# The first mixer's 31-tap convolution as column-packed products on TensorE

## Chip, cores, metric

One core of one Trainium2 chip. The metric is the device time of one execution in microseconds (us), the median of several runs. The engines are TensorE (PE, its weight loads PEld), VectorE (DVE), ScalarE (ACT), GpSimd (POOL) and SyncE (SP, which issues nearly all DMA).

## What is computed

A decoder trunk of two layers on 512 tokens of 1024 features, float32. Layer 0 runs sliding-window attention and a Conformer convolution side by side, each on its part of one input projection; their outputs, 512 + 512 features, go through one output projection. A gated feed-forward with a short convolution follows; layer 1 is a state-space mixer with the same feed-forward. Every residual is modulated by vectors computed from a condition c. The part that the change concerns:

```python
def conformer_conv(u, conv_w, conv_b, ln_g, ln_b):
    a, g = jnp.split(u, 2, axis=-1)                        # 512 features each
    h = causal_dwconv(a * jax.nn.sigmoid(g), conv_w, conv_b)  # 31 taps per feature
    mu = jnp.mean(h, axis=-1, keepdims=True)
    var = jnp.mean(jnp.square(h - mu), axis=-1, keepdims=True)
    h = (h - mu) * lax.rsqrt(var + LN_EPS) * ln_g + ln_b
    return jax.nn.silu(h)

merged = jnp.concatenate([attn, conf], axis=-1)            # attn: 8 heads, window 128
x = x + g_m * (merged @ w_out)
```

## The kernel before

The residual `x` stays on chip, feature-major: 8 tiles of 128 features by 512 tokens. A dense product takes three passes in a rounded float32 form: weights and inputs are split into a head and a remainder, and head by head, head by remainder and remainder by head are summed in PSUM (`mm3`, `product`). Weight tiles of 128 x 1024 stream from DRAM in the order of use (`Stream`): SP loads (`raw`, three buffers), ACT makes the head (`head`), DVE or POOL the remainder (`rest`).

`even_layer` is the first mixer. First the norm and the modulation fill `hn`, and six PSUM banks `g0` take the input products for three of the four convolution tiles (values and gates). Then a planner takes over. `Plan` holds tasks, each with an engine, a cost in us, what it waits for and which buffers it takes and gives; whenever an engine of its model falls idle it emits the ready task with the highest rank, which is the longest chain of costs behind it plus a number from the table `MIXER0`. `plan.run(MIXER0)` so fixes the order of every engine's instructions and of the DMA issues. A task made by `either` may have several ways, on DVE or on POOL.

The plan covers: two products for the fourth convolution tile (a3, g3), the key, value and four query products; rotary steps on DVE; for each of four head pairs (`head_tasks`) two units of scores, maxima, exponents, transposes (`turn`), copies (`bring`) and values, then a merge; the convolution of four tiles; its layer norm (means, centring, squares, variances, `ln`, silu); the output projection, first its attention half for all eight feature tiles (`out_a`), then the convolution half for four of them (`out_c`); and beside it 24 modulation chunks (`plan_mods`), each a load of 128 x 1024 weights and a dot with the condition.

One convolution tile is 128 features x 512 tokens. `gated` makes its input `us`; the last tap starts `cv`; the other 30 taps are one task each: on DVE a multiply-add on `cv` with a shifted `us`, or on ACT a product and on POOL an add into `cv2`; `conv_sum` joins the two. The modulation dot is one DVE operation, or a POOL product and an ACT sum. The scores of a unit are built per kv group: a mask product, then two products on that group's 64 rows. After the plan `boundary` makes the last four feature tiles of the output projection, 256 tokens at a time, and the next phase's norm.

Of the kernel before, what the change touches and what calls it, by code (L numbers as in the profile page):

```python
# [16 lines left out]
F32 = mybir.dt.float32  # L17
# [50 lines left out]
SIDE_LAST = 20.0  # L68
# [7 lines left out]
MIXER0 = {'sigmoid': -25, 'square': 43, 'osq_add': 139, 'head': -111, 'tap0': -113, 'attn_h': -95, 'conv_h': 49, 'out_c': 138, 'gated': 6, 'rest': -110, 'values': 71, 'rope': 59, 'rstd': -51, 'mod_sum': 7, 'attn_l': 103, 'var': 150, 'turn': 139, 'mod_end': 90, 'exp': -81, 'bring': 30, 'conv_sum': 54, 'out_a': -98, 'osq': -83, 'mod_act': -104, 'mod_add': 39, 'mod_free': 120, 'normalize': 30, 'load': -25, 'product': -67, 'mean_row': -71, 'mod_dve': 105, 'tap': -30, 'recip': 12, 'ln': 23, 'centre': -33, 'residual': -119, 'maxima': 140, 'rstd_row': -150, 'conv_l': 97, 'mean': 47, 'rope_in': 80, 'v_bias': -29, 'mod_load': 105, 'mod_dot': -93, 'root': 30, 'rows': -61, 'rows_in': -80, 'v_turn': -20, 'v_in': 85, 'mod 2': 18, 'head 0': -16, 'mu': 62, 'keys': 64, 'conv 0': 4, 'head 1': 2, 'mod 1': -4, 'head 3': -14}  # L76
# [20 lines left out]
class Way:  # L97
    """One engine's way of doing a task; then is one more task that follows if this way is taken."""
# [109 lines left out]
def trunk(ctx: ExitStack, tc: tile.TileContext, xT_d, vecs_d, rows_d, dsk_d, pos_d, const_d, wss_d, wg0_d,  # L208
          w_d, wmod_d, wdt_d, out_d):
# [34 lines left out]
    # ------------------------------------------------------------------ constants and small inputs  # L244
# [28 lines left out]
    # ------------------------------------------------------------------ splitting and products  # L273
# [4 lines left out]
    class Stream:  # L278
        """The weight tiles in the order in which they are used: DMA runs furthest ahead, then the
        split into heads and remainders, then the products."""  # L280
# [45 lines left out]
        def plan(self, plan, count, bonus, more):  # L326
# [51 lines left out]
    def spread(col, n=NCH):  # L378
        """[128 tokens, n] -> [128 partitions, n * 128 tokens], the same on every partition."""
# [15 lines left out]
    def rstd_cols(ss, width, e=0, n=NCH):  # L395
        """(sum / width + eps) ** -0.5 per token: ACT's square root, reciprocal, one Newton step."""
# [17 lines left out]
    def modulator(G, sh):  # L414
        """The normed, modulated, split tiles of the next phase, and what fills one token half."""
# [118 lines left out]
    # ------------------------------------------------------------------ modulation  # L534
# [6 lines left out]
    def condition(cp):  # L541
        """silu(c) on every partition."""
# [79 lines left out]
    def even_layer(lp, cp):  # L622
# [1205 lines left out]
```

## Time and profile before

| | |
|---|---|
| median of 3 runs | 1429.57 us (1427.97 to 1430.26) |
| profiled execution: span | 1428.4 us |
| PE busy | 1333.0 us (93%) |
| DVE busy | 969.4 us (68%) |
| ACT busy | 612.8 us (43%) |
| POOL busy | 339.1 us (24%) |
| DMA, mean over the span | 125 GB/s |

The span runs from the first to the last instruction; the profile gives no other time of its own for this execution, and the median of the runs stands 1.2 us above it. The shares are averages over stages with different limits. The page's 40 slices of 35.7 us show two kinds: PE is at nine tenths or more from the eighth slice on, and lower, with DVE at nine tenths, in the third to sixth. Views of single stretches, of groups of instructions by line, of waits, and the timeline give what happens there.

### The profile page before, as it was taken

To read this page: it belongs to the slowest core of one execution; us is meant where nothing else is said; L and a number is where in the kernel's file an instruction comes from. 1 tells how busy PE (TensorE), PEld (TensorE's weight loads), DVE (VectorE), ACT (ScalarE), POOL (GpSimd) and SP (SyncE) were. 2 spreads that over 40 slices of the span, in tenths; PEclk is the share of its full clock that TensorE was granted. 3 is DMA by queue.
4 is the path that set the end of the run, shared out by engine and by line. 5 is a ranking of instruction groups with operands and counts; after the bars stand their busy time and mean duration, and the time that the engine had idled before them with its cause. 6 is when DMAs were issued, how large, how long until landed. Compare 5 with 4: busy or idle time off the path is not lost. (4 is left out here: it accounts for less than half of the span.)

```text
span 1428.4 us, 17187 instructions
## 1 busy us (share of the span) xinstructions
PE 1333.0 (93%) x6574; PEld 1096.4 (77%) x6575; DVE 969.4 (68%) x1406; ACT 612.8 (43%) x897; POOL 339.1 (24%) x230
## 2 busy tenths in 40 slices
PE   6958748999999999999997999989999999999997
PEld 5745436888888888888786777777898888888886
DVE  7899999777566566657697866876766434444543
ACT  4545755454223323336467263464544322322333
POOL 7875767100000000011344422433210000000002
PEclk8977869999999999999998999999999999999998
DMA  8632016337566465432342332333214223223221
GB/s 302 246 117 89 1 57 208 113 128 231 162 206 197 148 221 191 147 102 86 117 133 85 115 114 74 135 95 100 88 40 139 90 89 114 85 92 108 92 70 59
DMA packets 54305, 178.08 MB, mean 125 GB/s; under 512 B 6480, under 2 KB 11088, under 8 KB 54224
## 3 DMA queue, kind: packets, MB, share of 16 engines
q1 hardware_dynamic: 53504, 176.34, 38.2%
q8 instruction: 51, 0.84, 0.2%
q10 hardware_dynamic: 688, 0.66, 0.2%
q14 instruction: 30, 0.25, 0.0%
q0 software_dynamic: 32, 0.00, 0.0%
HBM read 174.81 MB, written 2.16 MB: 124 GB/s over the span
## 5 line engine op out<-in xcount | busy, mean ns | idle before, releaser
L350 PE MATMUL ps<-hn,wl 128*128 128x512 f32 (+1 forms) x1214 | 458.1, 377 | 9.4 <-DVE wl L302 9.2
L348 PE MATMUL ps<-hn,wh 128*128 128x512 f32 (+1 forms) x1214 | 464.1, 382 | 1.1 <-ACT hn L424 0.8
L349 PE MATMUL ps<-hn,wh 128*128 128x512 f32 (+1 forms) x1214 | 458.2, 377 | 0.4
L297 ACT CAST wh<-raw 128x1024 fp32r<-128x1024 f32 (+1 forms) x208 | 213.0, 1027 | 206.4 <-PE ps L349 178.4
L302 DVE TENSOR_TENSOR wl<-raw,wh 128x1024 fp32r<-128x1024 f32 (+1 forms) x170 | 216.2, 1275 | 93.4 <-ACT wh L297 92.5
L350 PEld LDWEIGHTS ps<-hn,wl 128*128 128x128 f32 x1214 | 231.0, 190 | 52.5 <-DVE wl L302 10.4
L348 PEld LDWEIGHTS ps<-hn,wh 128*128 128x128 f32 x1214 | 231.6, 191 | 44.9 <-issue 2.0
L349 PEld LDWEIGHTS ps<-hn,wh 128*128 128x128 f32 x1214 | 231.2, 190 | 43.0 <-issue 1.7
L412 POOL TENSOR_TENSOR ssq<-ssq,tmp 128x512 f32<-128x512 f32 x10 | 13.3, 1334 | 725.0 <-ACT tmp L411 725.0
L437 DVE SCALAR_TENSOR_TENSOR x<-ps,modv,x 128x512 f32<-128x512 f32 (+1 forms) x108 | 74.2, 689 | 125.5 <-PE ps L350 125.3
L348 PE MATMUL ps<-fh,wh 128*128 128x512 f32 (+1 forms) x380 | 142.2, 374 | 0.0
L349 PE MATMUL ps<-fl,wh 128*128 128x512 f32 (+1 forms) x380 | 141.9, 373 | 0.0
L350 PE MATMUL ps<-fh,wl 128*128 128x512 f32 (+1 forms) x380 | 141.9, 373 | 0.0
L302 POOL TENSOR_TENSOR wl<-raw,wh 128x1024 fp32r<-128x1024 f32 x38 | 94.5, 2488 | 167.5 <-ACT wh L297 156.6
L566 DVE SCALAR_TENSOR_TENSOR mr<-mr,cb 128x1024 f32<-128x1024 f32 x86 | 117.8, 1375 | 0.0
L811 POOL TENSOR_TENSOR mr<-mr,tmp 128x506 f32<-128x506 f32 (+26 forms) x55 | 79.3, 1453 | 37.3 <-ACT tmp L806 35.1
L1224 DVE SCALAR_TENSOR_TENSOR tmp<-ps,vecs,tmp 128x511 f32<-128x511 f32 x44 | 32.9, 749 | 79.9 <-ACT tmp L1223 79.9
L1223 ACT ACTIVATE tmp<-ps,vecs 128x512 f32<-128x512 f32 x44 | 34.3, 780 | 115.4 <-PE ps L350 115.4
L348 PEld LDWEIGHTS ps<-fh,wh 128*128 128x128 f32 x380 | 71.5, 188 | 12.8
L349 PEld LDWEIGHTS ps<-fl,wh 128*128 128x128 f32 x380 | 71.5, 188 | 12.6
L350 PEld LDWEIGHTS ps<-fh,wl 128*128 128x128 f32 x380 | 71.5, 188 | 12.6
L796 DVE SCALAR_TENSOR_TENSOR s<-s,vecs,s 128x503 f32<-128x503 f32 (+28 forms) x61 | 74.7, 1236 | 1.2
(283 smaller groups left out, 1732.3 us busy)
## 6 DMA issues: line engine op xcount, KB each, us to landing
raw<-in_w_dram SPq DMA_DIRECT2D x176, 512.0 KB, 3.6
mr<-in_wmod_dram SPq DMA_DIRECT2D x80, 512.0 KB, 3.6
raw<-in_w_dram SPq DMA_DIRECT2D x32, 448.0 KB, 3.4
mr<-in_wss_dram SPq DMA_DIRECT2D x16, 512.0 KB, 6.2
M<-scr SPq DMA_DIRECT2D x16, 512.0 KB, 4.4
raw<-in_wg_dram SPq DMA_DIRECT2D x8, 384.0 KB, 4.7
E<-scr SPq DMA_DIRECT2D x32, 96.0 KB, 3.6
x<-in_xT_dram SPq DMA_DIRECT2D x8, 256.0 KB, 4.7
```

The source lines that it names most:

```text
L297: nc.scalar.copy(h, self.raw[i].rearrange("p (k m) -> p k m", m=P))
L302: eng.tensor_tensor(l, self.raw[i].rearrange("p (k m) -> p k m", m=P), h.bitcast(F32), ALU.subtract)
L348: mm(ps, lhsT=w[0], rhs=ah, start=first, stop=False)
L349: mm(ps, lhsT=w[0], rhs=al, start=False, stop=False)
L350: mm(ps, lhsT=w[1], rhs=ah, start=False, stop=last)
L412: nc.gpsimd.tensor_tensor(acc, acc, t_, ALU.add)
L437: stt(x[:, m, hs], ps, gate(m), x[:, m, hs], ALU.mult, ALU.add)
L566: stt(raw, raw, 1.0, mod_pool[2], ALU.mult, ALU.mult, accum_out=out)
L796: stt(cv[i][:, d:], us[i][:, :T - d], vec("ccw", i * 31 + k), cv[i][:, d:], ALU.mult, ALU.add)
L811: pool.tensor_tensor(cv2[i][:, d:], cv2[i][:, d:], st["tap", i, k][:, :T - d], ALU.add)
L1223: act(c, pg, AF.Identity, bias=vec("fcb", i), scale=vec("fcw", 3 * i + 2))
L1224: stt(c[:, 1:], pg[:, :T - 1], vec("fcw", 3 * i + 1), c[:, 1:], ALU.mult, ALU.add)
```

## The change

The taps leave DVE, ACT and POOL. `gated` is unchanged; its result goes to a DRAM scratch row of 544 columns per feature (`rows_c`: 30 zeros, 512 tokens, 2 zeros, the zeros written once by eight small DMAs), and comes back as four tiles of 128 partitions (`conv_fetch`): partition 32s + c holds feature c of a group of 32, shifted by s tokens (s = 0 to 3), 540 columns wide. One product over these 128 partitions with a matrix of 32 columns sums four taps for 32 features; eight of them, at column offsets of 4, sum 32 taps (the 32nd is zero). The four groups of 32 features write the four quarters of one PSUM bank (`tile_position`). The matrices, 512 KB a tile, are laid out on the host (`wcv`) and loaded into modulation buffers. The products are plain float32. ACT adds the bias (`cbias`).

Besides: the remainders, the dots and the splits of the merged tiles in this mixer are DVE's alone; the scores' products alternate between the kv groups; tile buffers, planner costs and the table `MIXER0` are new, so the whole order of the mixer is. Line numbers move by a few; comments are gone. (The table is shown by its first entries.)

```diff
@@ constants
-CONV_SIDE_N = 12
-CONV_SIDE = tuple(range(1, 29, 2))[:CONV_SIDE_N]
+CTAPS, CQ = 4, 8
+CPAD = 30
+CROW = CPAD + 512 + 2
+CWIN = 512 + CTAPS * (CQ - 1)
...
-MIXER0 = {'sigmoid': -25, 'square': 43, ...
+N_S = 26
+MIXER0 = {'sigmoid': -134, 'square': 32, ...
@@ Stream.plan
-                    t = plan.either("rest", [Way("DVE", 1.14 * n, lambda i=i: self.rest(i, nc.vector)),
-                                     Way("POOL", 2.3 * n, lambda i=i: self.rest(i, nc.gpsimd))],
-                                    [t], None, dict(raw=1), bonus)
+                    ways = [Way("DVE", 1.2 * n, lambda i=i: self.rest(i, nc.vector))]
+                    if pool:
+                        ways.append(Way("POOL", 2.3 * n, lambda i=i: self.rest(i, nc.gpsimd)))
+                    t = plan.either("rest", ways, [t], None, dict(raw=1), bonus)
@@ plan_mods
-            dots.append(plan.either("mod_dot", [
-                Way("DVE", 1.16, lambda st=st, n=n: mod_dot(st["r"], mod_at(n))),
-                Way("POOL", 2.35, lambda st=st: nc.gpsimd.tensor_tensor(st["r"], st["r"], mod_pool[2], ALU.mult), None, -SIDE_LAST,
-                    ("ACT", 1.04, lambda st=st, n=n: act(st["r"], st["r"], AF.Copy, accum_out=mod_at(n)), {}))],
-                [loaded], None, dict(mr=1)))
+            dots.append(plan.add("mod_dot", "DVE", 1.22, lambda st=st, n=n: mod_dot(st["r"], mod_at(n)),
+                                 [loaded], None, dict(mr=1)))
@@ even_layer
+        rows_c = [dp0.tile([P, CROW], F32, name=nm("uc")) for _ in range(4)]
...
+                for r_ in rows_c:
+                    nc.sync.dma_start(r_[:, 0:CPAD], zeros)
+                    nc.sync.dma_start(r_[:, CPAD + T:], zeros[:, 0:CROW - CPAD - T])
...
-        plan = Plan(dict(PE=2.3, DVE=1.8, POOL=0.5, DMA=2.5), ps=8 - NG0, tmp=6, mr=4 - len(early), units=UNITS, **W.room())
-        tiles = W.plan(plan, 16, 3.0, NEXT)
+        plan = Plan(dict(PE=2.3, DVE=1.8, POOL=0.5, DMA=2.5), ps=8 - NG0, tmp=6, mr=6 - len(early), u4=2, units=UNITS, **W.room())
+        tiles = W.plan(plan, 16, 3.0, NEXT, False)
...
-        def tap_dve(i, k):
-            d = 30 - k
-            stt(cv[i][:, d:], us[i][:, :T - d], vec("ccw", i * 31 + k), cv[i][:, d:], ALU.mult, ALU.add)
-
-        def tap_side(i, k):
...
-            act(st["tap", i, k][:, :T - d], us[i][:, :T - d], AF.Copy, scale=vec("ccw", i * 31 + k))
...
-                pool.tensor_tensor(cv2[i][:, d:], cv2[i][:, d:], st["tap", i, k][:, :T - d], ALU.add)
+        def conv_store(i):
+            nc.sync.dma_start(rows_c[i][:, CPAD:CPAD + T], us[i])
+        def conv_taps(i):
+            st["cw", i] = mod_raw().rearrange("p (g q c) -> p g q c", g=4, q=CQ)
+            nc.sync.dma_start(st["cw", i], wcv_d[i])
+        def conv_fetch(i):
+            u4 = st["u4", i] = [tile_s((P, CWIN)) for _ in range(4)]
+            src = rows_c[i][:, :]
+            for g in range(4):
+                nc.sync.dma_start(u4[g], bass.AP(src.tensor, src.offset + 32 * g * CROW,
+                                                       [[1, CTAPS], [CROW, 32], [1, CWIN]]))
+        def conv_product(i):
+            o = st["co", i] = bank()
+            for n in range(CQ):
+                for g in range(4):
+                    mm(o[32 * g:32 * g + 32, :], lhsT=st["cw", i][:, g, n, :], rhs=st["u4", i][g][:, 4 * n:4 * n + T],
+                       start=(n == 0), stop=(n == CQ - 1), tile_position=(0, 32 * g))
+        def conv_bias(i):
+            cv[i] = tile_s()
+            act(cv[i], st["co", i], AF.Identity, bias=vec("ccb", i))
...
-            taps = [plan.either("tap", [Way("DVE", 0.65, lambda k=k: tap_dve(i, k)),
-                                 Way("ACT", 0.6, lambda k=k: tap_side(i, k), dict(tmp=1), -SIDE_LAST,
-                                     ("POOL", 1.2, lambda k=k: tap_add(i, k), dict(tmp=1)))],
-                                [c_], bonus=20.0 - 0.3 * n) for n, k in enumerate(range(29, -1, -1))]
-            conv_done[i] = plan.add("conv_sum", "DVE", 0.6, lambda: tt(cv[i], cv[i], cv2[i], ALU.add) if sided[i] else None, taps)
+            d_ = plan.add("taps", "DMA", 1.8, lambda: conv_taps(i), [a_], dict(mr=1))
+            c_ = plan.add("store", "DMA", 1.0, lambda: conv_store(i), [b_])
+            c_ = plan.add("shifts", "DMA", 3.6, lambda: conv_fetch(i), [c_], dict(u4=1))
+            c_ = plan.add("conv", "PE", 7.4, lambda: conv_product(i), [c_, d_], dict(ps=1), dict(mr=1, u4=1))
+            conv_done[i] = plan.add("cbias", "ACT", 0.69, lambda: conv_bias(i), [c_], None, dict(ps=1))
@@ Unit.scores
                 for kv in range(2):
-                    half = slice(64 * kv, 64 * kv + 64)
-                    ps = bank((P, 2, 2 * P))
-                    mm(ps, lhsT=identb, rhs=maskb[:, min(bp, 1)], start=True, stop=False)
-                    for i in range(2):
...
+                    self.sps.append(bank((P, 2, 2 * P)))
+                    mm(self.sps[kv], lhsT=identb, rhs=maskb[:, min(bp, 1)], start=True, stop=False)
+                for i in range(2):
...
+                    for kv in range(2):
+                        half = slice(64 * kv, 64 * kv + 64)
+                        mm(self.sps[kv][:, i, 2 * P - nk:], lhsT=st["r", ("q", j)][half, b * P:(b + 1) * P],
                            rhs=st["r", "k"][half, k0 * P:(b + 1) * P], start=False, stop=(i == 1))
@@ two
-            return plan.either(label, [Way("DVE", cost, lambda: fn(nc.vector)),
-                                       Way("POOL", 2.05 * cost, lambda: fn(pool))], after, take, give)
+            return plan.add(label, "DVE", cost, lambda: fn(nc.vector), after, take, give)
```

How the order moves. DVE, from the first weight remainders of the plan on (`wl` a remainder, `mr` a modulation chunk in a dot, `s` of L786 and L789 the gated input, `s` of L790 and L796 the sum of taps), before:

```order
L566 SCALAR_TENSOR_TENSOR mr_508,modv<-mr_508,cb 128x1024
L786 SCALAR_TENSOR_TENSOR s_661<-ps_178,vecs,tmp_627 128x512
L786 SCALAR_TENSOR_TENSOR s_668<-ps_180,vecs,tmp_631 128x512
L786 SCALAR_TENSOR_TENSOR s_671<-ps_182,vecs,tmp_658 128x512
L302 TENSOR_TENSOR wl_666<-raw_499,wh_665 128x1024
L790 TENSOR_SCALAR s_679<-s_661,vecs 128x512
L302 TENSOR_TENSOR wl_675<-raw_585,wh_674 128x1024
L801 MEMSET mr_623 128x1
L796 SCALAR_TENSOR_TENSOR s_679<-s_661,vecs,s_679 128x510
L796 SCALAR_TENSOR_TENSOR s_679<-s_661,vecs,s_679 128x507
```

and in the change:

```order
L569 SCALAR_TENSOR_TENSOR mr_514,modv<-mr_514,cb 128x1024
L789 SCALAR_TENSOR_TENSOR s_676<-ps_190,vecs,tmp_641 128x512
L304 TENSOR_TENSOR wl_645<-raw_507,wh_644 128x1024
L789 SCALAR_TENSOR_TENSOR s_686<-ps_188,vecs,tmp_674 128x512
L789 SCALAR_TENSOR_TENSOR s_691<-ps_186,vecs,tmp_684 128x512
L304 TENSOR_TENSOR wl_679<-raw_601,wh_678 128x1024
L304 TENSOR_TENSOR wl_689<-raw_603,wh_688 128x1024
L569 SCALAR_TENSOR_TENSOR mr_516,modv<-mr_516,cb 128x1024
L569 SCALAR_TENSOR_TENSOR mr_518,modv<-mr_518,cb 128x1024
```

Where the taps of the first tile began now stand further remainders and dots.

SP at the same place, from the third early chunk on (`raw` a weight tile, `uc` the scratch rows, L742 and L743 their edges, L797 the tap matrices, L792 the store, L804 the shifted fetch), before:

```order
L558 DMA mr_512<-in_wmod_dram 128x1024
L289 DMA raw_585<-in_w_dram 128x1024
L289 DMA raw_587<-in_w_dram 128x1024
L558 DMA mr_663<-in_wmod_dram 128x1024
L289 DMA raw_681<-in_w_dram 128x1024
L558 DMA mr_711<-in_wmod_dram 128x1024
L289 DMA raw_726<-in_w_dram 128x1024
```

and in the change:

```order
L742 DMA uc_111<-zeros 128x30
L743 DMA uc_111<-zeros 128x2
L291 DMA raw_601<-in_w_dram 128x1024
L291 DMA raw_603<-in_w_dram 128x1024
L561 DMA mr_672<-in_wmod_dram 128x1024
L797 DMA mr_682<-in_wcv_dram 128x1024
L797 DMA mr_693<-in_wcv_dram 128x1024
L792 DMA uc_110<-s_676 128x512
L291 DMA raw_723<-in_w_dram 128x1024
L561 DMA mr_727<-in_wmod_dram 128x1024
L797 DMA mr_730<-in_wcv_dram 128x1024
L804 DMA s_761<-uc_110 128x1x540
```

Between the weight tiles stand the edge writes, the tap matrices and a store with its fetch.

PE, at a late unit of scores (L889/L892 the mask, L894/L899 the scores of one kv group each, L1035 a mean of the convolution, L937 a transpose), before:

```order
L889 LDWEIGHTS identb
L889 MATMUL ps_1386<-maskb,identb 128x512
L894 MATMUL ps_1386<-s_787,s_1275 128x128
L894 MATMUL ps_1386<-s_787,s_1275 128x256
L889 LDWEIGHTS identb
L889 MATMUL ps_1390<-maskb,identb 128x512
L894 MATMUL ps_1390<-s_787,s_1275 128x128
L894 MATMUL ps_1390<-s_787,s_1275 128x256
L1035 MATMUL ps_901<-s_903,ones 128x512
L937 MATMUL ps_1430<-con,s_1368 128x128
```

and in the change, at the unit after which the first convolution stands (L811):

```order
L892 LDWEIGHTS identb
L892 MATMUL ps_1143<-maskb,identb 128x512
L892 LDWEIGHTS identb
L892 MATMUL ps_1145<-maskb,identb 128x512
L899 MATMUL ps_1143<-s_777,s_1077 128x128
L899 MATMUL ps_1145<-s_777,s_1077 128x128
L899 MATMUL ps_1143<-s_777,s_1077 128x256
L899 MATMUL ps_1145<-s_777,s_1077 128x256
L811 MATMUL ps_1153<-s_761,mr_682 32x512
L811 MATMUL ps_1153<-s_762,mr_682 32x512
L811 MATMUL ps_1153<-s_763,mr_682 32x512
```

The scores' products now go to the two banks in turn, and the convolution is a run of 32 products on PE, three rows of which are shown.

## Rows read from the trace of the kernel before

**Rows 1.** Busy time by stretch: PE, PEld, DVE, ACT, POOL; clock, DMA share, GB/s.
```profile
0.00:63.84 63.84, 50.07 (x206) 40.10 (x207) 49.34 (x80) 32.11 (x55) 50.42 (x67) 0.89 0.74 263
63.84:265.98 202.14, 147.66 (x701) 107.58 (x701) 196.38 (x234) 108.36 (x219) 133.87 (x77) 0.81 0.32 105
265.98:300.00 34.02, 33.46 (x276) 32.97 (x275) 23.78 (x59) 17.05 (x32) 0.00 (x0) 1.00 0.32 117
```
**Rows 2.** Groups of DVE, 63.8 to 266: busy us, mean ns | idle before.
```profile
L796 DVE SCALAR_TENSOR_TENSOR s<-s,vecs,s 128x503 f32<-128x503 f32 (+28 forms) x61 | 74.7, 1236 | 1.2
L566 DVE SCALAR_TENSOR_TENSOR mr<-mr,cb 128x1024 f32<-128x1024 f32 x14 | 25.7, 1842 | 0.0
L302 DVE TENSOR_TENSOR wl<-raw,wh 128x1024 fp32r<-128x1024 f32 x10 | 20.9, 2109 | 1.1 <-ACT wh L297 1.1
```
**Rows 3.** Groups of POOL, 63.8 to 266.
```profile
L811 POOL TENSOR_TENSOR mr<-mr,tmp 128x506 f32<-128x506 f32 (+26 forms) x55 | 79.3, 1453 | 37.3 <-ACT tmp L806 35.1
```
**Rows 4.** Waits of PE, 63.8 to 266: us in total, times, longest.
```profile
PE ps L1035 <- DVE s L824: 17.1, 3, 11.6
PE ps L889 <- DVE s L796: 9.7, 1, 9.7
PE ps L350 <- DVE wl L302: 9.2, 2, 8.8
```
**Rows 5.** Groups of DVE, 300 to 400, shapes apart.
```profile
L302 DVE TENSOR_TENSOR wl<-raw,wh 128x1024 fp32r<-128x1024 f32 x20 | 24.5, 1223 | 7.1 <-ACT wh L297 7.1
L566 DVE SCALAR_TENSOR_TENSOR mr<-mr,cb 128x1024 f32<-128x1024 f32 x16 | 19.5, 1217 | 0.0
```
**Rows 6.** Timeline of PE: start us, us, what; the stage's first and last borders.
```profile
63.84 0.39 PE L348 MATMUL ps<-hn,wh 128*128 128x512 f32 x1
...
69.51 0.39 PE L349 MATMUL ps<-hn,wh 128*128 128x512 f32 x1
...
265.98 0.28 PE L348 MATMUL ps<-s,wh 128*128 128x256 f32 x1
```
**Rows 7.** Timeline of PE: attention and float32 products; x counts records.
```profile
157.92 0.93 PE L955 MATMUL ps<-s,s 128*64 128x128 f32 x12
158.78 1.09 PE L937 MATMUL ps<-con,s 128*128 128x128 f32 x8
159.80 1.14 PE L969 MATMUL ps<-con,sm 128*64 128x128 f32 x16
160.88 0.39 PE L889 MATMUL ps<-maskb,identb 128*128 128x512 bf16 x1
161.20 1.13 PE L894 MATMUL ps<-s,s 64*128 64x256 f32 x4
162.26 0.39 PE L889 MATMUL ps<-maskb,identb 128*128 128x512 bf16 x1
...
183.84 2.07 PE L1035 MATMUL ps<-s,ones 128*128 128x512 f32 x2 [5.08 <-DVE s L824]
185.71 3.18 PE L937 MATMUL ps<-con,s 128*128 128x128 f32 x14
...
217.56 3.73 PE L1026 MATMUL ps<-ones,tmp 128*128 128x1 f32 x32
```
**Rows 8.** Stretch of that float32 product; columns as in Rows 1.
```profile
183.84:185.70 1.86, 1.86 (x2) 0.73 (x3) 1.86 (x2) 0.00 (x0) 1.78 (x2) 0.50 0.44 95
```
**Rows 9.** Timelines of SP and ACT: a small load, the first plan loads, a split.
```profile
55.85 0.42 SPq L731 DMA_DIRECT2D rows<-in_rows_dram  x1
61.39 1.46 SPq L289 DMA_DIRECT2D raw<-in_w_dram  x2
69.86 1.05 ACT L297 CAST wh<-raw 128x1024 fp32r<-128x1024 f32 x1 [3.14 <-DMA raw<-in_w_dram]
```
**Rows 10.** The stretch with the backlog; columns as in Rows 1.
```profile
60.00:80.00 20.00, 19.40 (x85) 15.43 (x84) 19.80 (x21) 14.53 (x21) 15.95 (x7) 1.00 0.80 307
```
**Rows 11.** DMA issues: count, KB each, median us to landing.
```profile
raw<-in_w_dram SPq DMA_DIRECT2D x176, 512.0 KB, 3.6
```

More of the change, by code (lines that the diff above doesn't have):

```diff
@@ L75 @@
 N_XS, N_M, N_E = 8, 2, 2
-MIXER0 = {'sigmoid': -25, 'square': 43, 'osq_add': 139, 'head': -111, 'tap0': -113, 'attn_h': -95, 'conv_h': 49, 'out_c': 138, 'gated': 6, 'rest': -110, 'values': 71, 'rope': 59, 'rstd': -51, 'mod_sum': 7, 'attn_l': 103, 'var': 150, 'turn': 139, 'mod_end': 90, 'exp': -81, 'bring': 30, 'conv_sum': 54, 'out_a': -98, 'osq': -83, 'mod_act': -104, 'mod_add': 39, 'mod_free': 120, 'normalize': 30, 'load': -25, 'product': -67, 'mean_row': -71, 'mod_dve': 105, 'tap': -30, 'recip': 12, 'ln': 23, 'centre': -33, 'residual': -119, 'maxima': 140, 'rstd_row': -150, 'conv_l': 97, 'mean': 47, 'rope_in': 80, 'v_bias': -29, 'mod_load': 105, 'mod_dot': -93, 'root': 30, 'rows': -61, 'rows_in': -80, 'v_turn': -20, 'v_in': 85, 'mod 2': 18, 'head 0': -16, 'mu': 62, 'keys': 64, 'conv 0': 4, 'head 1': 2, 'mod 1': -4, 'head 3': -14}
+N_S = 26
+MIXER0 = {'sigmoid': -134, 'square': 32, 'osq_add': 34, 'head': -75, 'tap0': -113, 'attn_h': 106, 'conv_h': 47, 'out_c': 124, 'gated': 56, 'rest': 35, 'values': 23, 'rope': -136, 'rstd': 138, 'mod_sum': 7, 'attn_l': 28, 'var': -26, 'turn': 5, 'mod_end': 106, 'exp': -35, 'bring': -32, 'conv_sum': 54, 'out_a': -99, 'osq': -119, 'mod_act': -104, 'mod_add': 39, 'mod_free': 120, 'normalize': -150, 'load': -55, 'product': 71, 'mean_row': -71, 'mod_dve': 105, 'tap': -30, 'recip': 55, 'ln': 121, 'centre': 30, 'residual': -18, 'maxima': 26, 'rstd_row': 20, 'conv_l': 108, 'mean': 47, 'rope_in': 141, 'v_bias': 101, 'mod_load': 69, 'mod_dot': -97, 'root': -10, 'rows': -58, 'rows_in': 61, 'v_turn': 7, 'v_in': -3, 'mod 2': 18, 'head 0': 104, 'mu': -68, 'keys': 27, 'conv 0': 16, 'head 1': -47, 'mod 1': -115, 'head 3': -150, 'shifts': -127, 'scores': 66, 'mod 0': 94, 'conv 3': -77, 'conv 2': 93, 'cbias': -51, 'conv': -113, 'store': -126, 'taps': -47, 'conv 1': 18, 'head 2': 150}
 NG0 = 6
@@ L324, in room, with plan @@
             return dict(raw=3 - len(self.raw) + len(self.hl), hl=5 - len(self.hl) + self.taken)
-        def plan(self, plan, count, bonus, more):
+        def plan(self, plan, count, bonus, more, pool=True):
             out, last, prev = [], None, None
@@ L636, in even_layer @@
         nc.scalar.dma_start(con, const_d[:, 0:2 * P + 8])
+        zeros = lp.tile([P, CPAD], F32, name="zeros", tag="zeros", bufs=1)
+        nc.gpsimd.memset(zeros, 0.0)
         for kt in range(KT):
@@ L773, in emit @@
                 st[name] = product(W.hl[i][2], hn)
-            return plan.add("product", "PE", 5.2, emit, [split_], dict(ps=1), dict(hl=1))
+            return plan.add("product", "PE", 5.45, emit, [split_], dict(ps=1), dict(hl=1))
         st = {}
@@ L853, in rope @@
             a_ = plan.add("rope_in", "ACT", 0.57, lambda: rope_in(name, col, scale), [after], dict(tmp=1), dict(ps=1))
-            return plan.add("rope", "DVE", 2.5, lambda: rope_out(name), [a_], dict(tmp=1), dict(tmp=2))
+            return plan.add("rope", "DVE", 2.8, lambda: rope_out(name), [a_], dict(tmp=1), dict(tmp=2))
         plan.group = "keys"
@@ L997, in head_tasks @@
             for u in units:
-                t = plan.add("scores", "PE", 1.75 + 0.45 * u.bp, u.scores, [kr_, q_[j]], dict(ps=2, units=1))
-                t = plan.add("maxima", "DVE", 1.6, u.maxima, [t])
-                t = plan.add("exp", "ACT", 1.9, u.exponents, [t], None, dict(ps=2), table="exp")
-                recips.append(plan.add("recip", "DVE", 0.25, u.reciprocals, [t]))
+                t = plan.add("scores", "PE", 1.15 + 0.25 * u.bp, u.scores, [kr_, q_[j]], dict(ps=2, units=1))
+                t = plan.add("maxima", "DVE", 1.7, u.maxima, [t])
+                t = plan.add("exp", "ACT", 3.0, u.exponents, [t], None, dict(ps=2), table="exp")
+                recips.append(plan.add("recip", "DVE", 0.33, u.reciprocals, [t]))
                 t = plan.add("turn", "PE", 0.9, u.turn, [t], dict(ps=2))
-                t = plan.add("bring", "ACT", 0.95, u.bring, [t], None, dict(ps=2))
+                t = plan.add("bring", "ACT", 1.07, u.bring, [t], None, dict(ps=2))
                 last = plan.add("values", "PE", 0.8 + 0.3 * u.bp, u.values, [t, v_, last], dict(ps=1) if u.bp == 0 else None, dict(units=1))
@@ L1096, in emit @@
                 st[key] = product(W.hl[tiles[i][0]][2][4 * (m % 2):4 * (m % 2) + 4], acts)
-            t = plan.add(label, "PE", 2.6, emit, ready + [tiles[i][1]], dict(ps=1), dict(hl=1) if m % 2 else None,
+            t = plan.add(label, "PE", 2.72, emit, ready + [tiles[i][1]], dict(ps=1), dict(hl=1) if m % 2 else None,
                          bonus=-0.01 * m)
-            return plan.add("residual", "DVE", 0.66, lambda: residual(st[key], m, gate), [t, ends[0]] + after, None,
+            return plan.add("residual", "DVE", 0.72, lambda: residual(st[key], m, gate), [t, ends[0]] + after, None,
                             dict(ps=1))
@@ L1709, in trunk @@
     with tc.tile_pool(name="cp", bufs=1) as cp:
-        with tc.tile_pool(name="l0", bufs=1) as lp:
+        with tc.tile_pool(name="l0", bufs=1) as lp, \
+                tc.tile_pool(name="dr0", bufs=1, space=bass.MemoryType.DRAM) as dp0:
             mod_pool[:] = [lp, 6]
-            start = even_layer(lp, cp)
+            start = even_layer(lp, cp, dp0)
         with tc.tile_pool(name="f0", bufs=1) as fp:
@@ L1786, in pack @@
     r["w"] = np.concatenate([t.reshape(-1) for t in stream])
+    cw = np.zeros((CTAPS * CQ, 512), np.float32)
+    cw[:31] = a["conf_conv_w"][0]
+    diag = np.zeros((4, CTAPS, 32, 4, CQ, 32), np.float32)
+    for c in range(32):
+        diag[:, :, c, :, :, c] = cw.reshape(CQ, CTAPS, 4, 4, 32)[..., c].transpose(2, 1, 3, 0)
+    r["wcv"] = diag.reshape(4, P, 4, CQ, 32)
     parts = {
@@ L1806, in pack @@
     return {k: np.ascontiguousarray(r[k]) for k in _ORDER}
-_ORDER = ["xT", "vecs", "rows", "dsk", "pos", "const", "wss", "wg0", "w", "wmod", "wdt"]
+_ORDER = ["xT", "vecs", "rows", "dsk", "pos", "const", "wss", "wg0", "w", "wmod", "wdt", "wcv"]
 def kernel(**inputs):
```

37 lines of the change are left out of this document (8 added, 29 removed).

## The prediction

> **What bounds the kernel now.** I read the page first, for the stage in which the engines differ: the first mixer. Then busy time by stretch [rows 1]: in the 202.1 us from 63.84 to 265.98, in which the first mixer's planned order runs, VectorE (DVE) is busy 196.4 us (97%), TensorE (PE) 147.7 and at a granted clock of 0.81, a mixture of its two levels, 1.2 and 2.4 GHz. In the stretch behind it PE is busy 33.5 of 34.0 us at clock 1.00. So before 265.98 DVE sets the time, and from there PE does. The borders are two PE rows [rows 6]: the first product of the plan starts at 63.84, the first 256-column product of `boundary`, which follows the plan, at 265.98. Whatever moves this second row moves the end by as much, as long as the work behind it stays as it is; it does, by the diff.
>
> Next, what fills DVE [rows 2]: 61 convolution taps, 74.7 us; 14 modulation dots, 25.7 us; 10 weight remainders, 20.9 us. Beside it GpSimd (POOL) runs the adds of 55 more taps, 79.3 us [rows 3]. The same two DVE shapes, taken at 300 to 400 us where POOL stands still, last 1.217 (+0.083 for the accumulator) and 1.223 us [rows 5], against 1.842 and 2.109 in the mixer. POOL's work thus costs DVE 0.6 to 0.9 us in each of those. Last, PE's waits in the mixer [rows 4]: the three longest are all on DVE results (17.1 for the last sums of the convolution, 9.7 and 9.2 where a tap or a remainder came late); PE, idle or at the low clock, follows DVE.
>
> **What leaves, what comes.** DVE loses the taps and takes over what POOL did beside them. Counted from the changed order, between the first products and the boundary DVE has 24 dots x 1.30 = 31.2, 16 remainders x 1.22 = 19.5, 5 rotary steps, 16 maxima, 12 residuals and the small rest, which I put at 58 from operations on 512 columns at 0.6 to 0.75 each (half of the 1024-column rows, or a little more). That is 109 us, all at the uncontended durations, as POOL is empty until the sums of squares behind the output projection. ScalarE loses 55 tap products and gets 4 bias copies. Neither can set a stage longer than 109 us, so the next bound is PE, which gains the convolution.
>
> PE's sum at full clock, in one line of work after the other:
> - 8 input products of 24 matmuls: 25 steps from 63.84 to 69.51 are 0.227 each [rows 6], 43.5 us. 12 output products of 12 matmuls, 32.7.
> - The convolution: 4 tiles x 32 float32 matmuls of 512 columns with 32 output rows. Price of one: a float32 matmul of 512 columns takes 185.71 - 183.84 = 1.87 us [rows 7] at clock 0.50, the 1.2 GHz level [rows 8], so at most 0.94 at 2.4 GHz. The next point is whether four column groups run side by side. The trace has products with 64 output rows, which go to the array's two column halves in the order a a b b: 8 of them take 160.88 - 159.80 = 1.08 us, 6 take 158.78 - 157.92 = 0.86 (order a b a a b b) [rows 7]; there each product is two records. If a product waits only for the one before it in its own half, these orders need 5 and 4 slots, 0.216 and 0.215 us each: a float32 product of 128 columns. One after the other they would be 8 and 6 slots, 1.73 and 1.29 us. So halves run side by side in full, and 512 columns cost 0.86. In the change the groups go 0 1 2 3 0 1 2 3, which needs 8 slots: 6.9 us a tile, 27.6 in all. No row shows four groups. Bounds: below, this 27.6, since no row shows a product faster than its columns; above, no overlap at all, 32 x 0.86 x 4 = 110. I take 27.6, as the rows of halves lie exactly on it.
> - Scores: a mask product, then two products per kv group: 160.88 to 161.20 to 162.26, 0.32 + 1.06, and 0.32 + 0.85 where one product is a slot shorter. The change issues the kv groups alternately, each in its own 64 rows. Row halves side by side are not in the trace. If they overlap as column halves do: 4 heads x (0.64 + 0.85 + 0.64 + 1.06) = 12.8; if not, 20.4. I take 12.8.
> - Turns, 14 records a head at (159.80 - 158.78)/8 = 0.128 [rows 7]: 7.1. Values, 0.86 + 1.08 a head: 7.8. Row broadcasts 1.08 a head: 4.3. Means of the convolution 4 x 0.86 = 3.4, variances 3.6 [rows 7], two small ones 1.0.
>
> Sum 143.8 us.
>
> **Where PE still waits.** I followed the changed order from 63.84 on, with the trace's durations, engine by engine; three waits stay. (a) The loads. In the trace the fourth weight tile is issued at 61.39 and its split starts at 69.86 after waiting 3.14 us for the data [rows 9]: the queue works off a backlog at 307 GB/s [rows 10], 1.7 us per 512 KB. In front of this tile the change puts 8 small DMAs that clear the edges of the scratch rows: SP needs 0.42 us to issue one, 3.4 in all [rows 9], most of which the backlog covers. I bound their price by 0 and 3.4 and take 1.7: the tile comes at 71.5, the next at 73.2. Its remainder ends at 76.2 behind two others on DVE, so the third product stands 1.4 us, and the fourth ends at 87.0. (b) Behind these tiles the queue has two more modulation chunks, three tap matrices, one store and one set of four shifted fetches (1.1 MB) and two weight tiles. SP holds loads back too: a chunk waits for the dot that frees its buffer, and the loads behind it in SP's queue wait with it; here the backlog is longer than those waits. The sixth tile lands at 80.9, its split is ahead of the key's rotary input on ScalarE, the two rotary steps (four operations of 512 columns, 2.8 each) end at 90.1: the first scores stand 3.2 us. (c) The seventh tile lands at 91.3, split and remainder end at 93.6: 1.5 us. After that each operand is ready 3 us or more before PE's turn, the shifted rows too: the first set lands at 88 and is used near 120, the last is fetched when the second convolution frees its buffers, near 145, and is used near 163. So the 7.5 MB of taps, stores and fetches cost nothing there, since DMA was at 0.32 of its time in this stage [rows 1]; without that cover a fetch set would cost 3.6 us. At the end, behind the last mean, four centrings and a square (3.6 us) stand against 3.0 us of attention products, with one row copy between them: 1.2 us.
>
> Waits together 7.3. New start of the boundary: 63.84 + 143.8 + 7.3 = 214.9, instead of 265.98: **51 us** earlier. The profiled execution's span is 1428.4, 1.2 below the median of the runs, 1429.57; I subtract from the median: 1378.6, forecast **1379 us**.
>
> **The rivals.**
> Four groups overlap in part. For it: the rows of halves say nothing of four; against: they show no loss at all. With three groups' worth of work at a time a tile takes 32/3 slots of 0.86, 9.2 us, 9.2 more in all: **1388**. The Trainium skill, "TensorE: Matmul & The Clock Gate", Part 3 (packing small matmuls), speaks for this one: it gives 2.38 times for three column tiles, 0.79 of full overlap. The halves of this trace disagree, they overlap in full. With that share a tile would take an estimated 8.7 us and the kernel 1386.
> Only two groups at a time. For it: the trace shows two, no more. Against: the two were exact, with no sign of a limit. 16 slots a tile, 13.8 us, 27.6 more: **1406**.
> The first half stays fed by DMA and SP. All 24 dots are now on DVE, their buffers are shared with the tap matrices, and SP issues in order, so a late dot holds the weight tile behind it. If four tiles (the sixth to the ninth) each come late by one landing, split and remainder, 3.6 [rows 11] + 1.05 + 1.22 = 5.9, PE loses 23.5: **1402**. For it: the loads are on the path from 70 to 94 already. Against: the queue is FIFO and has work all that time, which SP's waits don't interrupt.
> Slower than before: the column groups don't overlap with four weight tiles of 32 columns in turn. Place: the four convolutions on PE; 32 x 0.86 = 27.5 instead of 6.9 each, 82.5 more, **1461**. It decides from the point where a convolution takes over 6.9 + 51/4 = 19.7 us, that is under 1.4 groups at a time. Against it are the halves; for it, that no row has four.
> It doesn't do what it says: DVE stays the bound in spite of 109 us, because POOL's share of the port was not what stretched its rows. With 24 x 1.92 + 16 x 2.11 + 58 x 1.5 = 167 us DVE would still be under 202: 167 + 7 gives 1401 at worst, so this isn't a case with a time of its own but lies in the range.
>
> **How the numbers follow.** Forecast 0.57, with its own range 1368 to 1392 (upwards the unpacked scores' 7.6 and 6 us more of waits, downwards none of the 7.3 us of waits, and 3 us for the measurement). Loads 0.13, three groups 0.12, two groups 0.08, slower 0.08, no change 0.02. The range reaches over the first four, whose upper end is 1406, and leaves out 0.10 and the forecast's tails: 1368 to 1407. Faster by over 0.2% 0.90, the same within 0.2% 0.02, slower by over 0.2% 0.08; 0.2%, 3 us, is about what a measurement of this kernel can tell from no change.
>
> **What would show it.** One convolution: 32 matmuls in about 6.9 us at clock 1.00; 9.2, 13.8 or 27.5 mean the rivals. Dots at 1.22 and remainders at 1.22 in the mixer. PE's first 256-column product near 215, its clock from 95 to there near 1.00, DVE busy about 109 of 151 us. PE idle before the first scores, little of it afterwards. The forecast is wrong if the row at 215 comes late with convolutions of 6.9 us: then the waits were mis-sized, and the time before 95 us against that behind it says whether it was the loads. It is wrong in another way if the stretch behind the boundary, 1162 us, isn't the same length.

## The result and the profile after

The change makes the kernel faster: 1407.71 us (1405.89 to 1409.59) against 1428.99 us, ratio 0.9848, 95% interval 0.9833 to 0.9863. That is 21 us instead of the 51 forecast, and 0.7 us above the upper end of the range. The profiled span is 1404.1 us, 24.3 less than before.

The same three stretches as in [rows 1], in the profile of the changed kernel (us and, for each engine, busy time and instructions; then granted clock, DMA share, GB/s). The border is again the first 256-column product, now at 245.66:

```profile
0.00:63.56 63.56, 50.85 (x206) 40.89 (x207) 49.45 (x87) 30.87 (x53) 48.81 (x67) 0.89 0.74 263
63.56:245.66 182.10, 154.57 (x958) 103.51 (x957) 99.14 (x183) 69.29 (x148) 4.71 (x3) 0.92 0.52 159
245.66:1404.00 1158.34, 1133.09 (x5670) 946.89 (x5668) 721.64 (x1094) 472.17 (x623) 151.77 (x86) 0.99 0.38 121
```

DVE's 196.4 us are down to 99.1, so it no longer sets the time. By the prediction PE needed 151.1 us for the stretch (143.8 of work and 7.3 of waits); it took 182.1. The prediction named the place to look in that case: if the convolutions take 6.9 us and the border still comes late, the waits were mis-sized. The first and the middle two convolutions, and the scores of a unit (two masks, then eight products), in the timeline:

```profile
142.53 7.07 PE L811 MATMUL ps<-s,mr 128*32 128x512 f32 x64
160.37 13.94 PE L811 MATMUL ps<-s,mr 128*32 128x512 f32 x128
158.77 0.60 PE L892 MATMUL ps<-maskb,identb 128*128 128x512 bf16 x2
159.30 1.14 PE L899 MATMUL ps<-s,s 64*128 64x256 f32 x8
```

Four column groups overlap in full, 6.94 us a tile (from the start of the middle pair to the next product, halved), and row halves too. So it is the waits. PE's waits in the stretch (us in total, times, longest), and ScalarE's and DVE's for DMA:

```profile
PE ps L351 <- ACT wh L299: 13.8, 2, 12.6
PE ps L973 <- ACT tmp L841: 7.1, 1, 7.1
PE ps L941 <- ACT s L921: 4.6, 4, 2.5
ACT wh L299 <- DMA raw<-in_w_dram: 42.5, 5, 18.4
DVE mr L569 <- DMA mr<-in_wmod_dram: 38.5, 4, 13.6
```

PE waits 27.6 us (1.2 and 0.9 in two more rows), each time behind a load; the 4.6 come by way of VectorE, where a dot waited 12.1 us for its chunk and held the maxima behind it back. The two longest follow two weight heads on ScalarE (start, duration, [idle before, ended by]); the third row is the first one's issue by SP:

```profile
102.16 1.04 ACT L299 CAST wh<-raw 128x1024 fp32r<-128x1024 f32 x1 [18.44 <-DMA raw<-in_w_dram]
126.73 1.04 ACT L299 CAST wh<-raw 128x1024 fp32r<-128x1024 f32 x1 [10.39 <-DMA raw<-in_w_dram]
87.08 0.56 SPq L291 DMA_DIRECT2D raw<-in_w_dram  x1
```

The first of these tiles was issued at 87.08 and used at 102.16: 15 us for 512 KB. What was DMA doing? Four short stretches of the changed kernel:

```profile
84.00:88.00 4.00, 4.00 (x19) 3.34 (x18) 3.97 (x10) 0.00 (x0) 0.00 (x0) 1.00 0.34 108
90.00:98.00 8.00, 0.66 (x8) 0.26 (x6) 0.00 (x0) 0.00 (x0) 0.00 (x0) 0.74 1.03 274
104.00:108.00 4.00, 3.96 (x11) 2.83 (x10) 3.93 (x9) 1.97 (x2) 0.00 (x0) 0.56 0.26 102
160.00:166.00 6.00, 6.00 (x61) 1.78 (x62) 1.20 (x2) 0.00 (x0) 0.00 (x0) 1.00 0.27 107
```

What matters are the last two columns. From 160 to 163 a fetch set runs almost alone, and to 166 what was queued behind it: the 16 engines are busy 0.27 of their time, so four of them work and twelve stand. The trace's records of single transfers say the same: the 512 rows of 2160 bytes of the first set start from 82.9 to 98.7 us and take 126 ns each in the mean, 64.7 us of work in 15.8 us, that is four at a time. From the first row's start to the last one's the four sets take 13.9 to 15.9 us. And at 104 to 108 the share is still 0.26, though no row of a set moves before 107.46: the records show rows of weights and of a store there, again about four at a time. Weight tiles are spread over all 16 engines. What fits these numbers is that twelve have long finished their part, that the last quarter waits its turn behind the rows on the other four, and that a tile has landed when this quarter has. (The records don't name their engine.)

Why four: the source of a fetch is written as 4 shifts of 32 features of 540 columns, so its outermost dimension is 4. The Trainium skill, "DMA: Bandwidth & Descriptors", section "Why a DMA increments its semaphore by 16 and not by 1", has the rule: a transfer takes the largest number of engines up to 16 that divides the outermost sizes of both sides. The trace agrees: 0.27 of 16 engines, four rows at a time.

### The profile page after: what moved, and what is told of

Its sections match the earlier page's. It is cut to its first block, busy times and chain, and to the rows that moved or that the text cites. A ratio compares the mean times of both kernels' runs of the same rounds, so it can differ in the third digit from the quotient of the medians.

```text
span 1404.1 us, 17533 instructions
## 1 busy us (share of the span) xinstructions
PE 1338.5 (95%) x6831; PEld 1091.3 (78%) x6831; DVE 870.2 (62%) x1363; ACT 572.3 (41%) x824; POOL 205.3 (15%) x156
## 5 line engine op out<-in xcount | busy, mean ns | idle before, releaser
L351 PE MATMUL ps<-hn,wh 128*128 128x512 f32 (+1 forms) x1214 | 462.2, 381 | 14.6 <-ACT wh L299 13.8
L569 DVE SCALAR_TENSOR_TENSOR mr<-mr,cb 128x1024 f32<-128x1024 f32 x96 | 122.5, 1284 | 38.6 <-DMA mr<-in_wmod_dram 38.5
L415 POOL TENSOR_TENSOR ssq<-ssq,tmp 128x512 f32<-128x512 f32 x10 | 13.3, 1332 | 724.9 <-ACT tmp L414 724.9
L304 POOL TENSOR_TENSOR wl<-raw,wh 128x1024 fp32r<-128x1024 f32 x31 | 74.7, 2410 | 166.0 <-ACT wh L299 163.1
L351 PEld LDWEIGHTS ps<-fh,wh 128*128 128x128 f32 x380 | 71.5, 188 | 12.6
L353 PEld LDWEIGHTS ps<-fh,wl 128*128 128x128 f32 x380 | 71.5, 188 | 12.6
L277 ACT CAST fh<-tmp 128x512 fp32r<-128x512 f32 x44 | 27.3, 621 | 96.4 <-DVE tmp L1230 96.4
L1228 ACT ACTIVATE tmp<-tmp 128x512 f32<-128x512 f32 x44 | 27.8, 633 | 74.9 <-DVE tmp L1227 74.9
```

What stands on the lines that cost most here:

```text
L277: nc.scalar.copy(h, src)
L304: eng.tensor_tensor(l, self.raw[i].rearrange("p (k m) -> p k m", m=P), h.bitcast(F32), ALU.subtract)
L351: mm(ps, lhsT=w[0], rhs=ah, start=first, stop=False)
L353: mm(ps, lhsT=w[1], rhs=ah, start=False, stop=last)
L415: nc.gpsimd.tensor_tensor(acc, acc, t_, ALU.add)
L569: stt(raw, raw, 1.0, mod_pool[2], ALU.mult, ALU.mult, accum_out=out)
```

## Experiments

Three theories. **F**: the fetches' four engines. **S**: SP's queue, that is the eight fills and the waits in its order. **O**: the planned order puts weight heads ahead of what PE needs on ScalarE.

**The fetches over 16 engines.**

```diff
-                                                       [[1, CTAPS], [CROW, 32], [1, CWIN]]))
+                                                       [[CROW, 32], [1, CTAPS], [1, CWIN]]))
...
-    diag = np.zeros((4, CTAPS, 32, 4, CQ, 32), np.float32)
+    diag = np.zeros((4, 32, CTAPS, 4, CQ, 32), np.float32)
-        diag[:, :, c, :, :, c] = cw.reshape(
+        diag[:, c, :, :, :, c] = cw.reshape(
```

> Theory F: a set of shifted fetches runs on only 4 of the 16 DMA engines, because the outermost dimension of its source is the 4 shifts; 512 rows of 126 ns are 64.5 us of work, 16.1 us on four engines, and every weight tile queued behind it is late by up to that. Here the same rows go in the order feature, then shift (outermost 32), and the weights' rows follow that order; bytes, instructions and their order stay. F expects a set to take about 4 us instead of 16, PE's waits of 12.6 us (at 90.7) and 7.1 us (at 121) to go with most of the half-clock time behind them, and 1380 to 1390 us. Theory S (SP's queue: the eight zero fills and the waits in SP's order make the loads late): no change, 1405 to 1410. Theory O (the planned order puts weight heads ahead of what PE needs on ScalarE): no change either.

Measured: 1379.87 us (1378.65 to 1381.32), ratio 0.9662 (0.9645 to 0.9678). F holds; S and O, which expected no change, fall as the cause: same bytes, same instructions in the same order, 28 us less. In its profile, the DMA stretch at 84, the stage, PE's waits in it, and the seventh weight tile's issue and head:

```profile
84.00:88.00 4.00, 4.00 (x19) 3.30 (x19) 3.96 (x10) 0.00 (x0) 0.00 (x0) 1.00 0.99 304
63.50:217.78 154.28, 149.79 (x961) 101.33 (x959) 99.96 (x187) 69.62 (x148) 4.72 (x3) 0.98 0.54 187
PE ps L351 <- ACT wh L299: 1.9, 2, 1.3
PE ps L353 <- DVE wl L304: 1.7, 2, 1.2
PE ps L899 <- DVE s L854: 0.8, 1, 0.8
83.73 0.38 SPq L291 DMA_DIRECT2D raw<-in_w_dram  x1
90.93 1.05 ACT L299 CAST wh<-raw 128x1024 fp32r<-128x1024 f32 x1 [7.11 <-DMA raw<-in_w_dram]
```

The sets take 3.7 to 4.6 us, some 12 rows at a time and not four. A row is no faster: between 84 and 87 us its median is 88 ns in both kernels. So the number at a time is what changed. The stage is 27.8 us shorter than with four engines: 23.2 in PE's waits (27.6 to 4.4) and 4.8 in PE's busy time (154.57 to 149.79), which is work at the low clock behind the waits: the granted clock is 0.98 over the stage instead of 0.92, and the stretch 104 to 108 above has 0.56. SP's long waits shrank as well: three weight loads in a row that took it 16.26 us to issue (from 115.87) took 7.68 (from 104.83). SP's order is the same in both kernels, so these waits followed from the late loads. They passed a part on: the seventh tile is issued 3.4 us later in the change (87.08 against 83.73), and from issue to use it takes 15.1 us instead of 7.2.

**Half of the fetches.** Two of the four fetches of a set spread, two as in the change.

```diff
+    [[CROW, 32], [1, CTAPS], [1, CWIN]] if g < 2 else [[1, CTAPS], [CROW, 32], [1, CWIN]]
```

> Two of a set's four fetches go by feature, then shift (16 engines), the other two as in the change (4 engines). Theory F: four engines carry 64 + 16 of the rows of a set each instead of 128, so a set takes 7 to 10 us instead of 16; the sixth weight tile comes 3 to 5 us later than with all fetches spread, some of the PE waits come back, and the time lies between: 1383 to 1394. If the number of small rows or of bytes set the price and not the engines, half of the gain: 1394; if any fetch on four engines spoils the stream, near the change, 1400 or more.

Measured: 1389.79 us (1386.95 to 1391.09). Between, as F has it; the sets take 10.3 to 13.3 us, longer than I expected: beside weight rows (88 to 94 us) a row takes 145 ns in the median, and 88 ahead of that. PE's longest wait:

```profile
PE ps L351 <- ACT wh L299: 8.4, 2, 7.9
```

**The fills early.** Two kernels: with the fetches as in the change, and spread.

```diff
@@ behind the memset of zeros
+        for r_ in rows_c:
+            nc.scalar.dma_start(r_[:, 0:CPAD], zeros)
+            nc.scalar.dma_start(r_[:, CPAD + T:], zeros[:, 0:CROW - CPAD - T])
```

> The eight zero fills are issued by ScalarE at the start of the kernel instead of by SP at 60 to 69 us; the fetches stay on four engines. Theory S expects the fourth weight tile 6 to 8 us earlier, the tiles behind it as well, and a gain of 8 us or more (under 1400). Theory F expects only the 2.4 us of PE's waits at 75 to 78 us to go, and this to be taken back by the wait for the sixth tile, which hangs on the first fetch set: 1405 to 1409.

> Both edits: fetches over 16 engines, fills early. Theory F: what the spread alone gives, and 2 to 3 us more, as PE's waits at 75 to 78 us now go for good: 1378 to 1387. Theory S: as the early fills alone.

Measured: 1406.13 us (ratio 0.9822 to 0.9865) and 1377.48 (0.9626 to 0.9655). With four engines the fills change nothing that can be told: PE's early wait moves to the next load, 11.2 us in one piece (below, first row). Spread and early together are 2.4 us under the spread alone, with overlapping intervals; ScalarE's eight issues came ahead of its first operations and its first weight heads moved from 59.38 to 62.78 (second row).

```profile
PE ps L353 <- DVE wl L304: 11.2, 1, 11.2
62.78 2.00 ACT L299 CAST wh<-raw 128x1024 fp32r<-128x1024 f32 x2
```

**No fetches.** GpSimd's zeros in their place.

```diff
-                nc.sync.dma_start(u4[g], bass.AP(src.tensor, src.offset + 32 * g * CROW,
...
+                nc.gpsimd.memset(u4[g], 0.0)
```

> The sixteen shifted fetches are left out; GpSimd fills the four buffers of each set with zeros, so the convolution's values are not computed, while its products, stores and tap matrices stay. Theory F: the fetches' cost is their four engines alone, so this is within 4 us of the spread fetches without early fills. A rival to F, that 1.1 MB of fetches in front of the weights are too much even at full width: 8 us or more faster than the spread fetches. Theory S: 1403 to 1409, since SP's order and the fills stay.

Measured: 1378.51 us (1377.36 to 1381.69), the spread kernel's time within the intervals. GpSimd's zeros don't stretch VectorE here: its dots take 1.216 us, 1.215 in the spread kernel. At full width 4.4 MB of fetches cost nothing that can be told, which is what the prediction had said of them.

**The order of the column groups.** Two kernels, both with spread fetches.

```diff
-            for n in range(CQ):
-                for g in range(4):
+            for g in range(4):
+                for n in range(CQ):
...
+            for g, n in [(2 * h + b, m) for h in range(2) for m in range(CQ) for b in range(2)]:
```

> The spread fetches, and the convolution's products of one group of 32 columns all in a row before the next group's (0 0 0 ... 1 1 1 ...). If a product waits only for the one before in its own column group, as the prediction had it, nothing overlaps now but at the three changes of group: 27 us a convolution instead of 7.0, 80 us more in all, about 1460. If the array takes any next product while one runs, no change.

> The spread fetches, and two column groups in turn (0 1 0 1 ..., then 2 3 2 3 ...). By the same rule two run at a time: 13.8 us a convolution instead of 7.0, 27 us more in all, about 1407, which is the second rival of the prediction made on purpose.

Measured: 1439.52 us (1436.96 to 1442.08) and 1396.81 (1393.33 to 1400.3), two runs each: 60 and 17 us more, the right direction and about a quarter and a third too small. The four convolutions take 88.5 and 47.1 us of PE's time, in the spread kernel 28.1. The first convolution of each, and the single group's records in equal stretches (time, busy, records):

```profile
122.75 22.59 PE L811 MATMUL ps<-s,mr 128*32 128x512 f32 x64
121.23 12.25 PE L811 MATMUL ps<-s,mr 128*32 128x512 f32 x64
122.74:127.45 4.71, 4.70 (x11) 1.00 0.52 182
127.45:132.20 4.75, 4.75 (x16) 1.00 0.96 326
```

Inside a group the price is what I took: 11 records in 4.71 us, 0.43 each, and two make a product, 0.86. Around a change of group 16 records start in 4.75 us: the next group's first products run beside the last ones of the group before. 64 records of 0.43 would be 27.5 us; 22.6 is 11 or 12 fewer, some 4 at each of the three changes. In pairs the one change saves likewise, 12.25 us instead of 13.8.

**The scores in the order of before**, with spread fetches.

```diff
-                for i in range(2):
...
-                    for kv in range(2):
+                for kv in range(2):
...
+                    for i in range(2):
```

> The spread fetches, and the scores' products in the order of before (one kv group after the other). If the row halves of the array run side by side as the prediction took them, the scores take 20.4 us instead of 12.8: 5 to 8 us more, 1385 to 1388. If they cost nothing or the change of order does nothing, 1380.

Measured: 1385.31 us (1382.35 to 1389.26), ratio 0.9694 (0.9672 to 0.9716), which just overlaps the spread kernel's. The rows decide: the row halves do run side by side. A kv group alone (first two rows) against both together (last two, spread kernel):

```profile
99.14 0.39 PE L893 MATMUL ps<-maskb,identb 128*128 128x512 bf16 x1
99.46 1.13 PE L898 MATMUL ps<-s,s 64*128 64x256 f32 x4
100.01 0.60 PE L892 MATMUL ps<-maskb,identb 128*128 128x512 bf16 x2
100.55 1.13 PE L899 MATMUL ps<-s,s 64*128 64x256 f32 x8
```

**GpSimd busy beside the mixer**, with spread fetches.

```diff
+        for _ in range(55):
+            pool.tensor_tensor(busy, busy, busy, ALU.add)
         plan.run(MIXER0)
```

> The spread fetches, with 55 additions of 512 columns on GpSimd beside the first mixer's start, whose result nobody uses, as many as the taps of before had. If GpSimd's work stretches VectorE's, dots and remainders beside it take 1.8 to 2.1 us instead of 1.22, VectorE's busy time in the mixer rises by 15 to 30 us, and with VectorE off the bound the time rises by far less: 1382 to 1392. If GpSimd was not the cause, they stay at 1.22 and the time at 1380.

Measured: 1400.96 us (1398.2 to 1402.79), 21 more, where I had expected 12 at most. DVE's dots and remainders from 64 to 150 us here, then in the whole stage of the spread kernel (count, busy us, mean ns):

```profile
L569 DVE SCALAR_TENSOR_TENSOR mr<-mr,cb 128x1024 f32<-128x1024 f32 x12 | 24.3, 2048 | 0.0
L304 DVE TENSOR_TENSOR wl<-raw,wh 128x1024 fp32r<-128x1024 f32 x11 | 20.4, 1860 | 0.0
...
L569 DVE SCALAR_TENSOR_TENSOR mr<-mr,cb 128x1024 f32<-128x1024 f32 x24 | 28.7, 1215 | 8.5 <-DMA mr<-in_wmod_dram 8.5
L304 DVE TENSOR_TENSOR wl<-raw,wh 128x1024 fp32r<-128x1024 f32 x16 | 19.4, 1220 | 4.5 <-PE ps L959 2.4 <-ACT wh L299 1.8
```

Two stretches of this kernel up to 150 us, in the columns of [rows 1]:

```profile
63.50:100.00 36.50, 27.03 (x108) 20.73 (x107) 32.83 (x37) 10.43 (x13) 34.70 (x24) 0.94 0.83 286
100.00:150.00 50.00, 42.93 (x252) 28.17 (x253) 49.03 (x60) 20.34 (x50) 45.15 (x31) 0.84 0.53 165
```

GpSimd's work alone stretches the two by 0.8 and 0.6 us. PE stands on the first heads' rotary steps (10.4 us in two waits for DVE's `s`) and works 9.5 us longer, at granted clock 0.92 over the stage. Over the stage DVE is busy for 134 of 176 us, which looks far from full; but beside the additions it is busy for 81.9 of 86.5 us, 95%, and there it is close to the bound again. I had sized the cost by the sum over the stage. The additions take back 21 of the 49 us that the spread kernel gains, so keeping GpSimd empty matters; they stand in one run at the start and not where the taps of before stood, so this is not the share of the gain that is due to the taps' going.

**The old cost in the second mixer.** In `Stream.plan` the change also set the planner's cost of a remainder from 1.14 to 1.2, and the second mixer is planned with it.

```diff
-                    ways = [Way("DVE", 1.2 * n, lambda i=i: self.rest(i, nc.vector))]
+                    ways = [Way("DVE", (1.14 if pool else 1.2) * n, lambda i=i: self.rest(i, nc.vector))]
```

> The spread fetches, with the planner's cost of a weight remainder set back from 1.2 to 1.14 where GpSimd may take it, that is in the second mixer alone; its order is then the one of before. If the 3.6 us that the stretch behind the boundary lost in the change come from this number: 3 to 4 us slower than the spread fetches, 1383 to 1384. If they come from somewhere else: 1380.

Measured: 1381.48 us (1379.01 to 1382.76), not to be told from 1379.87. Unsettled, see below.

**The best version.** Spread fetches; one more zero column in front and the unused weight first, so that four fills do; ScalarE issues them where it waits for GpSimd's angles.

```diff
-CPAD = 30
-CROW = CPAD + 512 + 2
+CPAD = 31
+CROW = CPAD + 512
@@ fifth input tile, behind drain(angle)
+                for r_ in rows_c:
+                    nc.scalar.dma_start(r_[:, 0:CPAD], zeros)
-    cw[:31] = a["conf_conv_w"][0]
+    cw[1:] = a["conf_conv_w"][0]
```

> The spread fetches, with four fills instead of eight (one zero column more in front and the unused 32nd weight first, so that no zeros are needed behind), issued by ScalarE at about 37 us, where it waits 3.5 us for GpSimd's angles. Fills early at the very start had delayed the first stage by 3.4 us, as ScalarE issued them ahead of its first operations; here the start should stay. Expected against the spread fetches alone: the fourth weight tile 3 us or more earlier, PE's waits from 75 to 94 us (4 us) gone, boundary near 214.5 and 1375 to 1377. If the loads bind anyway, as with the spread alone: 1380.

Measured: 1375.83 us (1373.1 to 1377.95), ratio 0.9621 (0.9606 to 0.9636), below the interval of the spread alone. The fourth tile's head starts at 70.81 instead of 73.04, the border is at 215.87 instead of 217.78. It beats both kernels, the changed one by 32 us. Of the 4.5 us of waits from 75 to 94 us only 1 is gone. Theory S thus has a small part: the fills cost up to 4 us with the fetches spread. Where all 4 went isn't shown: the border moved by 1.9, and the two profiled executions, this kernel's slowest and the spread kernel's fastest, differ by 0.7 us in their spans (1376.2 and 1376.9).

## Why the prediction was wrong, step by step

**The bound and its border** were right: DVE is off the path, and the first 256-column product moves the end. DVE's 109 us came out as 99.1, its dots at 1.218 and its remainders at 1.222 us, and the run with GpSimd busy shows that GpSimd was what stretched [rows 2].

**PE's sum** of 143.8 us met 149.8 busy in the spread kernel, 6 us too small. The packed parts hold: four convolutions 28.1 against 27.6, a unit's scores 1.40 and 1.60 against 1.49 and 1.70. Part of the rest is low clock: 0.79 granted from 90 to 98 us, behind the early waits, and 0.83 from 180 to 190. The second has no wait ahead of it: from 177.21 to 181.97 PE had done 16 products of one output column (the variances, 32 records), with 8 value products (16 records) among them, and the next eight products took 0.43 us each instead of 0.23, 1.6 us in all. The change and six of the other kernels show the same fall there. I had taken full clock from the first scores on. What the other part is stays open.

**Wait (a)**, 1.7 us for the eight fills with bounds of 0 and 3.4: the fourth tile's head came at 72.97, 3.1 later than [rows 9], inside the bounds, but SP took 8.3 us for the eight and not 3.4, as it waited 4.8 us for earlier loads between them. PE lost 2.4 us there, where I had 1.4. Mis-sized, small.

**Waits (b) and (c), and the sentence "each operand is ready 3 us or more before PE's turn"**: this is the step that failed: the price of a fetch set in the queue. I put a set into the queue as 1.1 MB at the queue's 307 GB/s, "without that cover a fetch set would cost 3.6 us". The four fetches run on four engines, a set holds these for 16 us, and everything queued behind it with them. So the sixth tile, taken at 80.9, had landed by 80.84, ahead of the fetches, and the first scores stood 0.9 us and not 3.2; the seventh, taken at 91.3, came at 102, and PE stood 12.6 us for it instead of 1.5; and the waits that followed, of 7.1 and 4.6 us, lay where I had forecast none. Of the 31 us by which the stage is longer than forecast, about 20 are waits and 5 low clock behind them; the other 6 are PE's sum. With the fetches spread PE's waits are 4.4 us where I had 7.3, the border comes at 217.78 (forecast 214.9), and the time is 1379.87 (forecast 1379). That it agrees to 1 us is partly luck: the sum is 6.0 us too small, the waits 2.9 too large, and the stretch behind the border 3.3 shorter than I took it. The cover that I named, DMA's 0.32 [rows 1], is a mean over 16 engines; it says nothing of a transfer that may use four.

**The rivals.** Nearest in time came "the first half stays fed by DMA and SP", 1402, and its place was right, not its mechanism: the fetches' engines came first, and late dots and SP's held issues followed from them. Part overlap (1388, and 1386 by the Trainium skill, "TensorE: Matmul & The Clock Gate", Part 3) fell: four groups show no loss, and the trace disagrees with that share. Two groups at a time, built as a kernel, cost 17 us where the rival had 27.6; one group at a time 60 where it had 82.5, since the changes of group overlap in both. That DVE stays the bound in the change is excluded by its 99 us; but what a stretched DVE costs I had sized by DVE's sum alone: with GpSimd busy DVE is at 134 of 176 us, and PE still pays 21, as DVE is at 95% until 150 us.

**Behind the border** I had taken 1162 us as unchanged "by the diff". From the border to the end of the span it is 1158.3 in the change, and 1156.4 to 1160.7 in the profiles of the other kernels with the new cost; with the old cost in the second mixer it is 1160.9, before 1162.4. The diff does reach there, through that cost: behind the border GpSimd runs 31 weight remainders with the new cost (spread kernel), 32 before and 32 with the old cost set back. Whether it explains the 4 us isn't settled: the spread between profiles of one order is as large.

## What to carry to other kernels

Before you put a transfer into a bandwidth sum, look at the outermost dimension of both its sides (the rule above; the runs here show it for the source, 4 against 32, with 128 at the destination): with 4 there, 1.1 MB take 16 us and not 4, and a weight tile queued behind them took 15 us from issue to use and not 7. In the profile this reads as a DMA share that stays near 0.25 while someone waits for DMA. Reordering partition rows, with the weights' rows laid out to match, mended it here with the same instructions.

## What was not expected of the hardware

- A weight tile that is spread over 16 engines is still used only 15 us after its issue when a fetch set holds four of them; DMA is at 0.26 of its time, 102 GB/s, 5 to 9 us after the set's last row.
- PE runs the first products of another column group beside the last ones of the group before: 16 records in 4.75 us, where a stretch inside a group has 11.
- In the spread kernel PE's granted clock fell right after 16 products of one output column (32 records), with no gap in PE's rows: 0.83 from 180 to 190 us.
- 55 additions on an otherwise unused GpSimd cost 21 us of 1380, with DVE busy for 134 of 176 us over the stage, but for 95% beside the additions.
